# A hybrid delta-rule and attention layer on one core: three steps given more planner ticks, and a pair's triangle scaled head by head

## The chip, the cores and the metric

The kernel runs on one core of a Trainium2 chip. The metric is the device time of one execution in microseconds (us). The engines are named as in the profile: PE is TensorE, PEld its weight loads, DVE is VectorE, ACT is ScalarE, POOL is GpSimd, SP is SyncE, which issues DMAs. L311 is line 311 of the kernel before.

## What is computed

One layer of a streaming encoder: 2048 frames of width 1024, with 16 learned meta tokens ahead of them. Two token mixers run on the same input, and their outputs are gated, merged, projected and normalised. Cut to its core, the reference is:

```python
q_a,k_a,v_a,z_a,beta,dec, q_b,k_b,v_b,z_b, gate_a,gate_b = split(h @ w_in)
# A: gated delta rule, 8 heads of 128, chunks of 64
lower = strict(k_beta @ k.T * decay)                 # a triangle for each chunk and head
u, w  = solve(lower + I, [v_beta, k_beta*exp(g)])    # its unit triangular inverse
for each chunk:  v_new = u - w @ S;  o = q_dec @ S + attn @ v_new;  S = S*gl + k_dec.T @ v_new
y_a = rmsnorm(o) * silu(z_a)
# B: window attention, 16 heads of 64, 4 key/value heads, meta tokens always visible
y_b = softmax(q_b @ k_b.T - alibi, sink) @ v_b * silu(z_b)
mixed = sigmoid(gate_a) * (y_a @ w_proj_a) + sigmoid(gate_b) * (y_b @ w_proj_b)
out = layernorm(alpha * h + mixed @ w_out)
```

## The kernel before, in words

The tokens run in four blocks of 512; the first also handles the meta tokens. Products in float32 are made of three products of high and low parts, so a projection of 128 outputs for 512 tokens (`proj`, L304) is 24 matmuls of 128x512 at L311, issued in four steps of six.

The order of all engines is written by a planner. `run` (L223) walks over a list of **fill**: the projections, step by step. Each step of the fill is one **tick**: the planner first runs what is due in the background (`bg`; a generator there that says `yield 3` goes on three ticks later), then lets up to two streams take a step, each at its own rate a tick. **chain** is the delta rule's recurrence for four groups of two heads (`stage_c`), then attention. **side** prepares the groups: the products of keys and the scaled triangle `LT` (`stage_b1`), and the scores of queries with `vtok` (`stage_b2`). The triangle's inverse, the meta tokens' heads and the output transposes (`stage_y`) run in the background. Between two groups the fill begins with `until(lambda: "vtok" in gr[g])`: it yields until side has made that group's `vtok`. These ticks hold no matmul of the fill; below they are **empty ticks**, and such a place is a **boundary**.

PE takes its instructions in the order written: a matmul of the fill that stands behind a waiting transpose waits as well. What isn't fill shares four PSUM banks (`bank()`, the pool `ps`), handed out in turn; a bank that still has a reader holds back who is next.

The lines that count below: L403, L404 and L406 write the meta tokens' keys in two copies (ACT) and their low part (DVE). L492 copies the first level of the meta triangle's inverse, and L497 multiplies with it. L807 is the product of keys, L815 the scaling of the triangle, L900 the last product of a group's inverse, L920 and L933 transposes of q and v, L723 the last step of the convolved v, L935 the scaling of the transposed v by `irk`, which DVE makes by some eleven tiny steps ahead of it (L160 to L169, L926; L937 follows). L960 to L994 is the recurrence; L971 multiplies by the state, L974 subtracts, L979 multiplies by the inverse, L984 scales, L992 updates the state. L962 adds a chunk's output, L965 sums its squares, L1001 and another such tiny chain make its norm, eight L1006 apply it, L1023 transposes the result. In attention, L1126 scales the probabilities, L1140 transposes them, L1142 keeps their high part, L1147 the low part, and L1156 to L1159 multiply them with the values; L1047 makes a low part of q.

Of the kernel before, what the change touches and what calls it, by code (L numbers as in the profile page):

```python
# [15 lines left out]
AF = mybir.ActivationFunctionType  # L16
# [3 lines left out]
P = 128  # L20
# [4 lines left out]
NC4 = TB // P  # L25
NM = 16
# [49 lines left out]
def hybrid_kernel(  # L76
# [26 lines left out]
    V, A, G, T, SY = nc.vector, nc.scalar, nc.gpsimd, nc.tensor, nc.sync  # L103
# [16 lines left out]
    def nm(s):  # L120
        cnt[0] += 1
        return f"{s}_{cnt[0]}"

    def g4(shape, dt=F32):
        return gp.tile(shape, dt, tag="g", name=nm("g"))

    def y4(shape, dt=F32):
        return gp.tile(shape, dt, tag="g", name=nm("y"))

    def s2(shape, dt=F32):  # L130
        return sp.tile(shape, dt, tag="s", name=nm("s"))

    def tiny(shape, tag, bufs=None):
        if bufs is None:
            bufs = 1 if tag[0] == "m" and tag not in ("mn", "mv") or tag[:2] == "gm" and tag[-1] not in "eg" else 2
        return tp.tile(shape, F32, tag=tag, name=nm(tag), bufs=bufs)

    def bank(pool=None):
        if pool is None:
            return pp.tile([P, 512], F32, tag="ps", name=nm("ps"))  # L140
        return pool.tile([P, 512], F32, tag="acc", name=nm("acc"))

    f = lambda ap: ap.bitcast(F32)
    def split_lo(out_, src, hi, pool=False):
        eng = G if pool else V
        eng.tensor_tensor(out=out_, in0=src, in1=f(hi), op=ALU.subtract)  # L146
# [4 lines left out]
    kmt = cp.tile([P, 2, KV, NM], F32R, name="kmt")  # L151
# [47 lines left out]
    def bg(gen, after=0):  # L199

        if after:
            clock["n"] += 1
            heapq.heappush(waiting, (clock["now"] + after, clock["n"], gen))
            return
        try:
            r = next(gen)
        except StopIteration:
            return
        if callable(r):
            def poll(r=r):  # L210
                while not r():
                    yield 3
                bg(gen)
            bg(poll())
            return
        bg(gen, r)
# [6 lines left out]
    def until(cond):  # L223
        while not cond():
            yield
# [172 lines left out]
    def meta_kb(u):  # L398
        def go(pf):
            for i in range(2):  # L400
                kv = 2 * u + i
                src = pf[64 * i:64 * i + 64, :NM]
                A.activation(kmt[0:64, 0, kv, :], src, AF.Copy)  # L403
                A.activation(kmt[64:128, 0, kv, :], src, AF.Copy)  # L404
                for a in (0, 64):
                    V.tensor_tensor(out=kmt[a:a + 64, 1, kv, :], in0=src, in1=f(kmt[64 * i:64 * i + 64, 0, kv, :]), op=ALU.subtract)  # L406
        return go
# [25 lines left out]
    def meta_heads(g, mstage, ok):  # L433
# [6 lines left out]
            out=gt,  # L440
            in0=tri[:NM, :NM].unsqueeze(1).to_broadcast([NM, 2, NM]),
# [21 lines left out]
        ncj = tiny([NM, 2], "mncj")  # L463
# [3 lines left out]
        pk = bank()  # L467
# [3 lines left out]
        LT = tiny([NM, 2, NM], "mLT")  # L471
# [16 lines left out]
        for lv in (1, 2, 3):  # L488
            pz = bank()
            for hh in range(2):  # L490
                T.matmul(pz[:NM, hh * NM:hh * NM + NM], M[:, lv, hh, :], W[:, 1, hh, :], start=True, stop=True)
            A.activation(Z, pz[:NM, 0:32].rearrange("p (h i) -> p h i", h=2), AF.Copy)  # L492
            yield 2
            n = 2 if lv < 3 else 1
            pw = bank()
            for hh in range(2):
                T.matmul(pw[:NM, hh * NM:hh * NM + NM], Z[:, hh, :], W[:, 0, hh, :], start=True, stop=True)  # L497
                if n == 2:
                    T.matmul(pw[:NM, 32 + hh * NM:32 + hh * NM + NM], W[:, 0, hh, :], Z[:, hh, :], start=True, stop=True)
            V.tensor_tensor(out=W[:, 0:n], in0=W[:, 0:n], in1=pw[:NM, 0:32 * n].rearrange("p (w h i) -> p w h i", w=n, h=2), op=ALU.add)  # L500
            yield 2
# [103 lines left out]
    def block(b, nextx):  # L605
# [174 lines left out]
        def stage_b1(g):  # L780

            d, h0 = gr[g], 2 * g
            beta, eg = gates["b"], gates["eg"]
            sk = tiny([P, 2, NC4], "sk")
            ktok = g4([P, 2, NC4, P])
            for hh in range(2):
                yield from until(lambda: ("ok", "kT", hh) in d)
                kT = d["kT"]
                pk = bank()
                for c in range(NC4):  # L790
                    T.transpose(out=pk[:, c * P:(c + 1) * P], in_=kT[:, hh, c * P:(c + 1) * P], identity=ident)
                A.activation(ktok[:, hh], pk, AF.Copy)
                for c in range(NC4):
                    A.activation(junk, pk[:, c * P:(c + 1) * P], AF.Square, accum_out=sk[:, hh, c:c + 1])
                yield
            LT = g4([P, 2 * NC4, P])
            cj = tiny([P, 2, NC4], "cj", 3)
            ncj = tiny([P, 2, NC4], "ncj")
            ce = tiny([P, 2, NC4], "ce", 3)
            yield from until(lambda: "E" in d)  # L800
            E = d["E"]
            yield
            pks = [bank() for hh in range(2)]
            for hh in range(2):
                for c in range(NC4):
                    kc = kT[:, hh, c * P:(c + 1) * P]
                    T.matmul(pks[hh][:, c * P:(c + 1) * P], kc, kc, start=True, stop=True)  # L807
            V.tensor_scalar(out=sk, in0=sk, scalar1=4e-6, scalar2=None, op0=ALU.add)
            V.reciprocal(out=cj, in_=sk)
            V.tensor_tensor(out=cj, in0=cj, in1=beta[:, :, h0:h0 + 2].rearrange("p c h -> p h c"), op=ALU.mult)  # L810
            V.tensor_scalar(out=ncj, in0=cj, scalar1=-1.0, scalar2=None, op0=ALU.mult)
            V.tensor_tensor(out=ce, in0=cj, in1=eg[:, 1, :, h0:h0 + 2].rearrange("p c h -> p h c"), op=ALU.mult)
            for hh in range(2):
                for c in range(NC4):
                    V.scalar_tensor_tensor(out=LT[:, hh * NC4 + c, :], in0=pks[hh][:, c * P:(c + 1) * P], scalar=ncj[:, hh, c:c + 1],  # L815
                                           in1=E[:, hh, c * P:(c + 1) * P], op0=ALU.mult, op1=ALU.mult)
            d.update(ktok=ktok, LT=LT, sk=sk, cj=cj, ce=ce)
            bg(inverse(g))
            yield
# [193 lines left out]
        def stage_y(g):  # L1013

            d = gr[g]
            yield lambda: ("ok", "zs", 1) in d
            yield 1
            o, zs = d["o"], d["zs"]
            gr[g] = None
            for hh in range(2):  # L1020
                pt = bank()
                for c in range(NC4):
                    T.transpose(out=pt[:, c * P:(c + 1) * P], in_=o[:, hh, c, :], identity=ident)  # L1023
                V.scalar_tensor_tensor(out=zs[:, hh, :], in0=pt, scalar=gw, in1=zs[:, hh, :], op0=ALU.mult, op1=ALU.mult)
                yield 2
            yield 2
            yh = y4([P, 2, TB], F32R)
            A.activation(yh, zs, AF.Copy)
            yield 5
            yl = y4([P, 2, TB], F32R)  # L1030
            split_lo(yl, zs, yh)
            ya.append((yh, yl))
# [99 lines left out]
        def swa_turn(ch, w):  # L1132

            s = w["starts"][ch]
            Pt = w["Pt"]
            kt = (208 - s) // 2
            pT = bank()
            for j in range(2):
                for rt in range(2):
                    T.transpose(out=pT[0:kt, j * 256 + rt * P:j * 256 + rt * P + P], in_=Pt[:, ch, rt, s + j * kt:s + j * kt + kt], identity=ident)  # L1140
            ph = s2([P, 512], F32R)
            A.activation(ph[0:kt], pT[0:kt], AF.Copy)  # L1142

            def end():
                yield 1
                pl = s2([P, 512], F32R)
                V.tensor_tensor(out=pl[0:kt], in0=pT[0:kt], in1=f(ph[0:kt]), op=ALU.subtract)  # L1147
                w["p", ch] = kt, ph, pl

            bg(end())  # L1150
# [127 lines left out]
        def project(nx):  # L1278
# [125 lines left out]
            def terms(acc, c, kq, k2, wh, wl, lo):  # L1404
# [4 lines left out]
                else:  # L1409
# [6 lines left out]

        chain = series(*(stage_c(g) for g in range(4)), swa())
        side = series(decays(), stage_b0(0), *(p_ for g in range(3) for p_ in (stage_b1(g), stage_b0(g + 1), stage_b2(g))),
                      stage_b1(3), stage_b2(3), swa_first())
        both = (chain, side)  # L1420
        run([tokens(), *stage_a(0), k_b(0), k_b(1)], both, (RATES[0], SIDE[0]))
# [3 lines left out]
        u = [p_ for kv in range(1, KV) for p_ in swa_proj(kv)]  # L1425
# [102 lines left out]
```

## Time and profile before

| what | us |
|---|---|
| three runs | 2647.66, 2648.50, 2649.97 (median 2648.50) |
| the profiled execution | 2648.3 |
| its span in the trace | 2646.5 |
| PE busy in it | 2608.6 (99%) |
| DVE, ACT, POOL busy | 1533.4, 1222.9, 772.8 |

The profiled execution has 1.8 us around its span. PE is busy nearly all the time, so the table of what PE waits for is the one to read; then the timeline of PE and DVE at the places where it waits. Busy time of modelled matmuls overlaps, so starts tell more than durations.

### The profile page before, as it was taken

How to read it: one execution, taken by the hardware profiler on the slowest of the kernel's cores; microseconds unless marked ns; L12 is line 12 of the kernel's file. 1: busy time of each engine (PE TensorE's matmuls, PEld its weight loads, DVE VectorE, ACT ScalarE, POOL GpSimd, SP SyncE). 2: the span in 40 equal slices, each digit the busy share in tenths (PEclk: the TensorE clock that was granted, in tenths of full speed). 3: DMA queues.
4: the chain of work that ended last, by engine and by line, in shares of the span. 5: the costliest groups of instructions: out<-in, count | busy, mean ns of one | idle time of the engine just before them, and what ended most of it. 6: DMA issues, size and time to landing. Idle time of an engine off the chain costs nothing.

```text
span 2646.5 us, 44333 instructions
## 1 busy us (share of the span) xinstructions
PE 2608.6 (99%) x15444; PEld 2173.8 (82%) x15444; DVE 1533.4 (58%) x3863; ACT 1222.9 (46%) x3260; POOL 772.8 (29%) x1792
## 2 busy tenths in 40 slices
PE   9999999999999999999999999999999999999998
PEld 7677878888888888888888888888888888888886
DVE  6667756763565554763465554676347456476435
ACT  4565545552245544653224554565323454365422
POOL 2554333532056330111116532010102753011022
PEclk9999999999999999999999999999999999999999
DMA  7655555653675454674466545476347644557533
GB/s 257 207 198 180 186 191 159 200 167 96 205 244 169 135 167 143 201 207 132 152 225 186 170 135 164 151 212 184 120 157 243 190 142 149 164 172 210 171 98 136
DMA packets 243136, 461.61 MB, mean 174 GB/s; under 512 B 77648, under 2 KB 135760, under 8 KB 242912
## 3 DMA queue, kind: packets, MB, share of 16 engines
q1 hardware_dynamic: 242912, 458.78, 54.4%
q8 instruction: 122, 2.00, 0.3%
q14 instruction: 102, 0.84, 0.1%
HBM read 379.87 MB, written 78.81 MB: 173 GB/s over the span
## 4 chain that ended last, share of the span: by engine, by line
PE 89%; DVE 6%; ACT 3%; DMA 1%; issue 1%; SPq 0%; POOL 0%; DVEq 0%; ACTq 0%
PE acc L311 63%; PE ps L1140 2%; PE ps L1105 2%; PE ps L915 1%; PE ps L960 1%; PE ps L807 1%; PE ps L971 1%; PE ps L1158 1%; PE ps L992 1%; PE acc L1408 1%; PE acc L1411 1%; PE acc L1410 1%; PE ps L979 1%; PE ps L981 1%; PE ps L1408 1%; PE ps L1411 1%
## 5 line engine op out<-in xcount | busy, mean ns | idle before, releaser
L311 PE MATMUL acc<-xh,wh 128*128 128x512 f32 x1800 | 735.2, 408 | 0.3 <-ACT wh L275 0.3
L311 PE MATMUL acc<-xl,wh 128*128 128x512 f32 x1800 | 705.4, 392 | 0.0
L311 PE MATMUL acc<-xh,wl 128*128 128x512 f32 x1800 | 480.7, 397 | 0.0
L275 ACT ACTIVATE wh<-wr 128x1024 fp32r<-128x1024 f32 (+1 forms) x246 | 258.4, 1050 | 281.6 <-PE acc L311 151.8
L311 PEld LDWEIGHTS acc<-xh,wh 128*128 128x128 f32 x1800 | 339.1, 188 | 60.1 <-issue 1.4
L311 PEld LDWEIGHTS acc<-xl,wh 128*128 128x128 f32 x1800 | 339.7, 189 | 57.1
L311 PEld LDWEIGHTS acc<-xh,wl 128*128 128x128 f32 x1800 | 329.1, 189 | 65.6 <-issue 0.5
L718 DVE SCALAR_TENSOR_TENSOR s<-st,cw,s 128x512 f32<-128x512 f32 x288 | 229.4, 797 | 108.2 <-ACT st L713 101.2
L311 PE MATMUL acc<-y,wh 128*128 128x512 f32 x1024 | 251.5, 392 | 0.0
L146 DVE TENSOR_TENSOR wl<-wr,wh 128x1024 fp32r<-128x1024 f32 (+2 forms) x125 | 161.9, 1295 | 149.7 <-ACT wh L275 128.6
L841 POOL TENSOR_TENSOR tm<-X,g 128x60 f32<-128x60 f32 (+24 forms) x496 | 163.1, 329 | 251.8 <-DMA g<-d 216.7
L311 PEld LDWEIGHTS acc<-y,wh 128*128 128x128 f32 x1024 | 188.5, 188 | 36.7
L311 PE MATMUL acc<-xh,wr 128*128 128x512 f32 x624 | 210.7, 402 | 0.0
L1257 POOL TENSOR_TENSOR g<-g 128x512 f32<-128x512 f32 x32 | 69.7, 2177 | 395.4 <-DVE g L1250 385.5
L843 POOL TENSOR_TENSOR X<-X,tm 128x60 f32<-128x60 f32 (+24 forms) x496 | 170.8, 344 | 38.8
L1142 ACT ACTIVATE s<-ps 104x512 fp32r<-104x512 f32 (+2 forms) x128 | 76.3, 597 | 153.3 <-PE ps L1140 137.3
L1250 DVE SCALAR_TENSOR_TENSOR g<-g,acc 128x512 f32<-128x512 f32 x64 | 44.0, 687 | 154.5 <-PE acc L311 154.5
L311 PEld LDWEIGHTS acc<-xh,wr 128*128 128x128 f32 x624 | 115.6, 188 | 21.5
L311 PE MATMUL acc<-y,wl 128*128 128x512 f32 x512 | 130.7, 392 | 0.0
L146 POOL TENSOR_TENSOR wl<-wr,wh 128x256 fp32r<-128x256 f32 x120 | 87.0, 756 | 137.4 <-ACT wh L275 116.6
L760 POOL TENSOR_TENSOR g<-cm,gh 128x256 fp32r<-128x256 f32 x64 | 53.9, 872 | 249.6 <-DVE gh L672 206.9
L1241 ACT ACTIVATE g<-acc,bg__162 128x512 f32<-128x512 f32 x64 | 44.1, 689 | 177.3 <-PE acc L311 171.0
(340 smaller groups left out, 4679.6 us busy)
## 6 DMA issues: line engine op xcount, KB each, us to landing
wr<-in_wfm_dram SPq DMA_DIRECT2D x214, 512.0 KB
wl<-ws SPq DMA_DIRECT2D x165, 512.0 KB
wr<-ws SPq DMA_DIRECT2D x78, 512.0 KB
wh<-ws SPq DMA_DIRECT2D x75, 512.0 KB
ws<-wl SPq DMA_DIRECT2D x68, 512.0 KB
g<-kd SPq DMA_DIRECT2D x240, 96.0 KB
ws<-wh SPq DMA_DIRECT2D x38, 512.0 KB
wr<-in_wo_dram SPq DMA_DIRECT2D x32, 512.0 KB
```

What stands on the lines that cost most here:

```text
L146: eng.tensor_tensor(out=out_, in0=src, in1=f(hi), op=ALU.subtract)
L275: A.activation(hi[:, k], raw[:, k], AF.Copy)
L311: T.matmul(ps, w_[:, k, :], r_(k), start=(n == 0), stop=(n == 3 * NK - 1))
L718: V.scalar_tensor_tensor(out=acc, in0=st[:, 3 - d:TB + 3 - d], scalar=cw[:, s, 3 - d:4 - d], in1=acc, op0=ALU.mult, op1=ALU.add)
L760: G.tensor_tensor(out=gt[:, hh, c:c + 2], in0=tri.unsqueeze(1).to_broadcast([P, 2, P]), in1=part[:, c:c + 2, h0 + hh:h0 + hh + 1].to_broad ...
L841: G.tensor_tensor(out=tm[:, :n, :r], in0=X[:, :n, j:j + 1].to_broadcast([P, n, r]), in1=L[:, j:j + 1, j + 1:].to_broadcast([P, n, r]), op= ...
L843: G.tensor_tensor(out=X[:, :n, j + 1:], in0=X[:, :n, j + 1:], in1=tm[:, :n, :r], op=ALU.add)
L1105: T.matmul(o_, d["q", rt][:, 2 * cp2 + ch], KX[:, l, ch, s:208], start=l == 0, stop=l == 1)
L1140: T.transpose(out=pT[0:kt, j * 256 + rt * P:j * 256 + rt * P + P], in_=Pt[:, ch, rt, s + j * kt:s + j * kt + kt], identity=ident)
L1142: A.activation(ph[0:kt], pT[0:kt], AF.Copy)
L1257: G.tensor_tensor(out=m[:, u % 2, :], in0=t[:, 0, :], in1=t[:, 1, :], op=ALU.add)
L1408: T.matmul(acc, ah, wl[:, k2, :], start=False, stop=kq == 3 and k2 == 1)
```

## The change

It has five edits. (1) The meta tokens' keys: all four copies on ACT first, then the four subtractions on DVE. (2) In the first group's meta triangle, three ticks instead of two after the copy of L492. (3) In `stage_b1` the tiny steps on DVE come ahead of the products, each head takes its bank apart, and between the scalings of the first head and those of the second lies one more step of side, so that the inverse and all later steps of side come one step later for each group. (4) The output transposes come three ticks after what they wait for, instead of one. (5) The probabilities' low part is published one tick after the subtraction.

```diff
     def meta_kb(u):
         def go(pf):
             for i in range(2):
+                for a in (0, 64):
+                    A.activation(kmt[a:a + 64, 0, 2 * u + i, :], pf[64 * i:64 * i + 64, :NM], AF.Copy)
+            for i in range(2):
                 kv = 2 * u + i
                 src = pf[64 * i:64 * i + 64, :NM]
-                A.activation(kmt[0:64, 0, kv, :], src, AF.Copy)
-                A.activation(kmt[64:128, 0, kv, :], src, AF.Copy)
                 for a in (0, 64):
                     V.tensor_tensor(out=kmt[a:a + 64, 1, kv, :], in0=src, ...)
@@ meta_heads, after the copy of L492
-            yield 2
+            yield 2 + (g == 0)
@@ stage_b1
-            pks = [bank() for hh in range(2)]
-            for hh in range(2):
-                for c in range(NC4):
-                    kc = kT[:, hh, c * P:(c + 1) * P]
-                    T.matmul(pks[hh][:, c * P:(c + 1) * P], kc, kc, start=True, stop=True)
             V.tensor_scalar(out=sk, in0=sk, scalar1=4e-6, ...)
 ...
             for hh in range(2):
+                pk = bank()
                 for c in range(NC4):
+                    kc = kT[:, hh, c * P:(c + 1) * P]
+                    T.matmul(pk[:, c * P:(c + 1) * P], kc, kc, start=True, stop=True)
+                if hh:
+                    yield
+                for c in range(NC4):
-                    V.scalar_tensor_tensor(out=LT[:, hh * NC4 + c, :], in0=pks[hh][:, c * P:(c + 1) * P], ...)
+                    V.scalar_tensor_tensor(out=LT[:, hh * NC4 + c, :], in0=pk[:, c * P:(c + 1) * P], ...)
             d.update(ktok=ktok, LT=LT, sk=sk, cj=cj, ce=ce)
             bg(inverse(g))
@@ stage_y, ahead of the output transposes
-            yield 1
+            yield 3
@@ swa_turn, end
                 V.tensor_tensor(out=pl[0:kt], in0=pT[0:kt], in1=f(ph[0:kt]), op=ALU.subtract)
+                yield 1
                 w["p", ch] = kt, ph, pl
```

Since the order is planned, the edits move more than the lines they touch. Lines of the changed kernel stand one to three further down (L971 is L973 there, L1023 is L1025). Its planner runs 1511 ticks instead of 1487, six more in each block, of which 36 instead of 12 are empty: four instead of two at each boundary of block 0, and four, two and two instead of two, none and none in each later block.

On PE at the third boundary of block 0, the kernel before ends the inverse, transposes v twice and goes on with the fill (`acc`; `cm` with a `g` is a transpose):

```order
L900 MATMUL ps_2935<-g_1520,s_2868 64x64 x8
L933 MATMUL ps_2967<-cm,g_2779 128x128 x4
L933 MATMUL ps_3012<-cm,g_2779 128x128 x4
L311 MATMUL acc_3028<-xh_101,wh_2849 128x512
L311 MATMUL acc_3028<-xl_102,wh_2849 128x512
```

On PE, four fill matmuls, the state's product L971 and four more of the fill later, it comes to the first output transposes:

```order
L311 MATMUL acc_3028<-xh_126,wh_2849 128x512
L311 MATMUL acc_3028<-xl_127,wh_2849 128x512
L317 MATMUL acc_3054<-wr_2692,xm 32x128 x8
L1023 MATMUL ps_3066<-cm,g_1140 128x128 x4
L311 MATMUL acc_3028<-xh_132,wh_2849 128x512
```

On PE at the same place, the changed kernel (L902 is before's L900, L922 its L920, L935 its L933; `S` is the state):

```order
L311 MATMUL acc_2831<-xh_132,wl_2708 128x512 x2
L902 MATMUL ps_2911<-g_1518,s_2847 64x64 x8
L922 MATMUL ps_2957<-cm,g_2518 128x128 x4
L935 MATMUL ps_2994<-cm,g_2769 128x128 x4
L973 MATMUL ps_3009<-S_86,g_1393 128x128 x2
L1025 MATMUL ps_3016<-cm,g_1157 128x128 x4
L935 MATMUL ps_3028<-cm,g_2769 128x128 x4
L311 MATMUL acc_3044<-xh_101,wh_2828 128x512
```

The output transposes now stand in the empty ticks, right behind the state's product, with no fill between them and the inverse's last product; the second half of v's transposes stands behind them.

On DVE in the fourth group of block 0, the kernel before ends the chain for `irk`, then v's last step (L723), then begins the norm of the outputs (L1001):

```order
L169 SCALAR_TENSOR_TENSOR irk_3881<-rst_3885,irk_3881 128x8
L926 TENSOR_TENSOR irk_3881<-irk_3881,sk_3076 128x8
L937 TENSOR_SCALAR sq_3661<-sq_3661 128x8
L723 SCALAR_TENSOR_TENSOR g_3797<-s_3875,s_3793 128x512
L1001 SCALAR_TENSOR_TENSOR so_3041<-so_3041,sq_1737 128x8
L160 TENSOR_SCALAR rsi_3928<-so_3041 128x8
```

On DVE at the same place, the changed kernel from the end of the norm's chain (`ro`) on:

```order
L169 SCALAR_TENSOR_TENSOR ro_3870<-rst_3874,ro_3870 128x8
L1008 TENSOR_SCALAR g_2000<-g_2000,ro_3870 128x128 x8
L160 TENSOR_SCALAR rsi_3899<-sk_3101 128x8
L161 TENSOR_SCALAR irk_3898<-rsi_3899 128x8
L167 SCALAR_TENSOR_TENSOR rst_3902<-sk_3101,irk_3898 128x8
```

On DVE, after six more rows of that chain:

```order
L169 SCALAR_TENSOR_TENSOR irk_3898<-rst_3902,irk_3898 128x8
L928 TENSOR_TENSOR irk_3898<-irk_3898,sk_3101 128x8
L939 TENSOR_SCALAR sq_3675<-sq_3675 128x8
L724 SCALAR_TENSOR_TENSOR g_3795<-s_3896,s_3789 128x512
L146 TENSOR_TENSOR wl_3850<-wr_3733,wh_3848 128x1024
```

The norm and its eight scalings (L1008) now stand ahead of the chain for `irk`, and v's last step (L724) stands last of all three.

On DVE at the start of attention in block 0, the kernel before (`ls` are the sums of the first and the second set of probabilities):

```order
L1121 TENSOR_TENSOR ls_5132<-ls_5132,m_949_5131 128x4
L1122 RECIPROCAL ls_5132<-ls_5132 128x4
L1126 TENSOR_SCALAR g_5129<-g_5129,ls_5132 128x80 x2
L1126 TENSOR_SCALAR g_5129<-g_5129,ls_5132 128x144 x2
L1047 SCALAR_TENSOR_TENSOR g_5238<-acc_5159,g_5238 64x8x64 x2
L1121 TENSOR_TENSOR ls_5193<-ls_5193,m_964_5192 128x4
L1122 RECIPROCAL ls_5193<-ls_5193 128x4
L1126 TENSOR_SCALAR g_5190<-g_5190,ls_5193 128x208 x4
L1147 TENSOR_TENSOR s_5289<-ps_5270,s_5275 40x512
```

On DVE at the same place, the changed kernel:

```order
L1049 SCALAR_TENSOR_TENSOR g_5232<-acc_5137,g_5232 64x8x64 x2
L1123 TENSOR_TENSOR ls_5150<-ls_5150,m_954_5149 128x4
L1124 RECIPROCAL ls_5150<-ls_5150 128x4
L1128 TENSOR_SCALAR g_5147<-g_5147,ls_5150 128x80 x2
L1128 TENSOR_SCALAR g_5147<-g_5147,ls_5150 128x144 x2
L1123 TENSOR_TENSOR ls_5199<-ls_5199,m_964_5198 128x4
L1124 RECIPROCAL ls_5199<-ls_5199 128x4
L1128 TENSOR_SCALAR g_5196<-g_5196,ls_5199 128x208 x4
L1149 TENSOR_TENSOR s_5295<-ps_5276,s_5281 40x512
```

The two steps for the low part of q (L1047, L1049 there) moved from between the two sets to ahead of both.

## Rows read from the trace of the kernel before

**Rows 1.** The page: its head, and part 1, busy time by engine.

```profile
span 2646.5 us, 44333 instructions
PE 2608.6 (99%) x15444; PEld 2173.8 (82%) x15444; DVE 1533.4 (58%) x3863; ACT 1222.9 (46%) x3260; POOL 772.8 (29%) x1792
```

**Rows 2.** PE's waits: its line, whom it waited for; total us, times, longest.

```profile
PE acc L629 <- ACT wh L275: 4.6, 1, 4.6
PE ps L992 <- DVE s L984: 3.1, 3, 1.0
PE ps L1158 <- DVE s L1147: 2.6, 5, 1.6
PE ps L915 <- ACT g L889: 1.8, 3, 0.6
...
PE ps L1023 <- DVE g L1006: 1.2, 1, 1.2
PE ps L1023 <- DVE s L1147: 1.1, 3, 0.4
...
PE ps L497 <- ACT g L492: 1.0, 1, 1.0
...
PE ps L979 <- ACT g L430: 0.8, 1, 0.8
...
PE acc L311 <- ACT wh L275: 0.3, 1, 0.3
```

**Rows 3.** Timeline, start of attention in block 0: start, us, engine, line, operation, tiles [idle before].

```profile
428.42 1.39 DVE L1047 SCALAR_TENSOR_TENSOR g<-acc,g 64x512 fp32r<-64x512 f32 x2
...
433.70 0.59 PE L1158 MATMUL ps<-s,s 40*64 40x256 f32 x2 [1.62 <-DVE s L1147]
...
434.43 2.93 PE L311 MATMUL acc<-xh,wl 128*128 128x512 f32 x6
```

**Rows 4.** Windows there: stretch, length, busy us by engine, PEclk, DMA share, GB/s.

```profile
433.80:437.30 3.50, 3.50 (x10) 2.69 (x11) 3.12 (x18) 0.00 (x0) 0.40 (x3) 0.51 0.85 283
```

**Rows 5.** Timeline, third boundary of block 1.

```profile
907.53 2.32 DVE L718 SCALAR_TENSOR_TENSOR s<-st,cw,s 128x512 f32<-128x512 f32 x3
...
910.25 0.68 PE L992 MATMUL ps<-s,g 128*128 128x128 f32 x4 [1.04 <-DVE s L984]
...
910.69 1.63 PE L311 MATMUL acc<-xh,wl 128*128 128x512 f32 x6
```

**Rows 6.** Timeline, third boundary of block 0.

```profile
229.09 0.29 DVE L416 TENSOR_TENSOR macc<-mstage,cw 128x32 f32<-128x32 f32 x1
...
230.71 1.34 DVE L146 TENSOR_TENSOR wl<-wr,wh 128x1024 fp32r<-128x1024 f32 x1
...
231.37 1.14 PE L900 MATMUL ps<-g,s 64*64 64x64 f32 x16
...
232.44 1.09 PE L933 MATMUL ps<-cm,g 128*128 128x128 f32 x8
...
232.91 0.17 DVE L160 TENSOR_SCALAR rsi<-sk 128x8 int32<-128x8 int32 x1
...
235.44 0.15 DVE L1001 SCALAR_TENSOR_TENSOR so<-so,sq 128x8 f32<-128x8 f32 x1
...
238.00 1.93 DVE L1006 TENSOR_SCALAR g<-g,ro 128x128 f32<-128x128 f32 x8
...
238.54 0.88 PE L1023 MATMUL ps<-cm,g 128*128 128x128 f32 x4 [1.21 <-DVE g L1006]
```

**Rows 7.** Timeline, fourth group of block 0.

```profile
300.40 0.30 DVE L424 SCALAR_TENSOR_TENSOR mkm<-mth,macc 128x32 f32<-128x32 f32 x1
...
303.94 0.70 DVE L723 SCALAR_TENSOR_TENSOR g<-s,s 128x512 f32<-128x512 f32 x1 [0.40 <-ACT s L721]
...
305.87 0.60 PE L933 MATMUL ps<-cm,g 128*128 128x128 f32 x4
```

**Rows 8.** All 128 of L815: ns min/median/max, first and last start, tiles.

```profile
L815 DVE SCALAR_TENSOR_TENSOR g<-ps,ncj,g x128: 335/342/353, 65.6 to 2209.9; 128x128 f32<-128x128 f32 x128
```

More of the change, by code (lines that the diff above doesn't have):

```diff
@@ L813, in stage_b1 @@
             for hh in range(2):
+                pk = bank()
                 for c in range(NC4):
-                    V.scalar_tensor_tensor(out=LT[:, hh * NC4 + c, :], in0=pks[hh][:, c * P:(c + 1) * P], scalar=ncj[:, hh, c:c + 1],
+                    kc = kT[:, hh, c * P:(c + 1) * P]
[3 more added lines that the diff above has]
+                for c in range(NC4):
+                    V.scalar_tensor_tensor(out=LT[:, hh * NC4 + c, :], in0=pk[:, c * P:(c + 1) * P], scalar=ncj[:, hh, c:c + 1],
                                            in1=E[:, hh, c * P:(c + 1) * P], op0=ALU.mult, op1=ALU.mult)
```

## Prediction

> **What bounds the kernel now.** I read the page first: PE is busy 2608.6 of 2646.5 us, and DVE, ACT and POOL are busy for less than 60% [rows 1]. So a change that adds no matmul can give back only what PE waits, and can cost only new waits. Then I read the table of PE's waits: of its nineteen rows, from 4.6 to 0.3 us and 25.2 us in all, the largest is the first weight at the program's start, which no edit reaches [rows 2]. Last I read the timeline where PE waits. Two things are to be seen there. Most waits last 1.2 us or less, and they are places where a chain of tiny steps on DVE or a copy on ACT is a little longer than the work that PE has ahead of it. One is longer: in block 0 the low part of the probabilities holds PE for 1.62 us, and right behind it six matmuls of the fill take 2.93 us [rows 3]. In that stretch the granted clock is 0.51, half of the full 2.4 GHz [rows 4]. Behind a wait of 1.04 us six such matmuls took 1.63 [rows 5], so that one brought no slow stretch. So this wait cost 1.62 us, and the slow clock some 1.3 to 1.7 more (2.93 less 1.63, or half of 3.50).
>
> **The change part by part.** Its 24 more ticks cost nothing by themselves: an empty tick holds no matmul, PE takes the next thing in its row. What counts is that each empty tick takes away six matmuls, 1.63 us of cover [rows 5], from whatever PE waits for next. I worked each place from the new order and the durations of the trace.
>
> Block 0, first boundary. The third tick after L492 and the copies in a new order put other work between the copy and L497. Its wait of 1.0 [rows 2] goes: **-1.0** (0 to -1.5; the other waits of that inverse may grow or go).
>
> Block 0, second boundary. L979 now follows closer on L974, which DVE reaches behind a chain of tiny steps. The nearest row is the wait at L979 for ACT, 0.8 [rows 2]: **+0.8** (0 to 1.5).
>
> Block 0, third boundary. In the new order DVE runs, from where the seven tiny steps of the meta convolution began (229.09), first L146 (1.34 [rows 6]), a 128x512 step (0.7, as L723 [rows 7]), then these seven (229.09 to 230.71, 1.62), then the norm's chain (235.44 to 238.00, 2.56) and eight L1006 (1.93) [rows 6]. So the first L1006 is done at about 235.5, the fourth at 236.3, the eighth at 237.2. PE comes to the output transposes after L900 (231.37, 1.07 to the next start) and twelve short matmuls or transposes (some 1.3; eight L933 took 1.09 [rows 6]), at 233.7. Instead of running until 234.1 they end at 236.4: 2.3 lost. Behind the norm DVE then makes `irk` (232.91 to 235.44, 2.53 [rows 6]) and L974 (two of some 0.34 as L815 [rows 8]), until 240.4. PE has four transposes and six matmuls for that time (0.5 and 1.63 [rows 5, 6]) and stands at L979 from 238.5 to 240.4: 1.9 lost. Edit (4) means to clear this, but its three ticks are empty ones here. Less the 1.21 of L1023 in the kernel before [rows 6]: **+3.0** (+1 to +6: the one end if DVE comes to the chain 2 us sooner, the other if the copies of L935, which free the bank that L979 takes, end later).
>
> Block 0, fourth group. The second half of v's transposes (L933 at 305.87, no wait) needs L723, done at 304.6 [rows 7]. In the new order DVE has the norm's chain, eight L1006 and the chain for `irk` first: from the end of L424 (300.7 [rows 7]) 2.56 + 1.93 + 2.53 [rows 6] + 0.7 [rows 7] = 7.7, so 308.4. PE has the same work ahead: **+2.6** (+1 to +5, since the squares that the norm needs may come later).
>
> Block 0, the clock. The last three of these waits are 2.3, 1.9 and 2.6 us long, and the only row for a wait of such a length had the half clock behind it [rows 3, 4]. One such stretch at 1.5 is in the sum (0 to 4.8, none or all three): **+1.5**. The Trainium skill, page "TensorE: Matmul & The Clock Gate", section "HAM oscillation — how this bites in real kernels", says that an engine that idles long enough between pieces of work falls to the low clock and works slowly again after each such gap, so that the price of a gap is more than the gap; that speaks against this change, which makes one gap into three. By that rule all three would pay, 3 us on top of my sum; the trace agrees with it at 433.70 [rows 3, 4], and shows no gap of this length without it.
>
> Block 0, attention. Here the reason that the 1.62 us go is not the tick of edit (5) but the shift of the whole plan: L1047 (1.39 [rows 3]) moved from between the two sets of probabilities to ahead of both, so L1147 stands 1.39 sooner behind its set. The wait falls to some 0.2, and with it the slow stretch: -1.4 - 1.6 = **-3.0** (-3.5 to 0: if other work on DVE moved into the gap, nothing is gained). The other four waits of L1158 (1.0 in all [rows 2]) and edit (5)'s tick give **-0.5** more. In the steady state a set passes every five ticks and the order of PE and DVE is the same as before, so this tick costs nothing: the transposes, scores and values of the sets around lie between as they did.
>
> Blocks 1 to 3, each. L992's wait of 1.0 goes, since the empty ticks shift the recurrence past the three L718 (2.32 us) that held L984 [rows 5], but one of about the same size comes at the same boundary, where L979 has two ticks less ahead of it and DVE still has a norm to make: 0. L915's wait of 0.6 goes [rows 2], and 0.3 of L1023's behind L1147 [rows 2]: edit (4) moves these transposes two ticks on. In the last group the split triangle has a cost: the bank for L979 is freed by L962, which DVE now reaches behind L146 (1.34 [rows 6]), L723 (0.7), five tiny steps (0.2 each, as the seven above) and the four scalings of the first head (4 x 0.342 = 1.37 [rows 8]), 4.4 us; PE has some 3.2 of fill and the eight products (1.1 if they take what eight L933 do [rows 6]) in that time, and DVE starts only when L971 has landed: +0.4 (0 to 1.2). The scalings of the second head, the inverse and the recurrence one step later cost nothing as long as the recurrence doesn't wait for its inverse; the fill covers that, but at a boundary nothing does (this is in the +0 to +1.2). Sum for a block **-0.5** (-1.5 to +2), for three **-1.5**.
>
> The sum: -1.0 + 0.8 + 3.0 + 2.6 + 1.5 - 3.0 - 0.5 - 1.5 = **+1.9**. The profiled execution took 2648.3 (2646.5 in the span [rows 1] and 1.8 around it), 0.2 under the median of 2648.5. So 2650.2.
>
> **The rivals.** *Slower, by the clock.* Each of the three new gaps of block 0 is followed by half clock as the one of 1.62 us was, and two of them stand at their upper ends: 3 x 1.6 instead of 1.5 (+3.3), +4.5 instead of +3.0, +4.5 instead of +2.6: 2650.2 + 6.7 = 2656.9. For it speak the rows at 433.70 [rows 3, 4]; against it that DVE may come to its chains earlier than I put it, since it is busy for 58% only. It decides from 3.6 us above my sum, which is two stretches of half clock and a little of the gaps.
>
> *Faster.* The orders at the boundaries are not as tight as I read them, no new wait forms, and the old ones go: 1.62 and 1.6 for the clock, 1.0 for L1158's others, 1.1 and 1.2 for L1023, 1.0 for L497, 1.8 for L915, part of L992's 3.1 (say 1) [rows 2]: -10.3, so 2638. For it speaks that each edit stands at a wait of the table; against it that the new ticks are empty ones just where the norm is late, and that nearly all of the list has to go to get 5.3.
>
> *The change doesn't do what it says.* The output transposes' ticks are empty, edit (5)'s leaves the order as it is, and the step of `stage_b1` is made up by side's rate; only small waits move about: 2648 to 2649.
>
> **How the numbers follow.** A measurement of this kernel can tell about 0.2% from no change, 5.3 us: under 2643.2 is faster, over 2653.8 slower. My forecast, new gaps in block 0 that just outweigh what goes, has 0.42; the rival without effect 0.20; slower by the clock 0.25; faster 0.13. The forecast's own bounds (2645 to 2654) lie within 0.2% but for a little, so: faster 0.13, same 0.61, slower 0.26. The range leaves out the far half of each of the two outer rivals: 2643.5 to 2657.
>
> **What would show it.** In the profile after: at the third boundary of block 0, waits of L1025 for L1008 and of L981 for L976 or L937 of about 2 us each; in the fourth group, one of L935 for L724 of 2 to 3 us; half clock behind at least one of them. The wait of L1161 for the low part at 433 gone, and PEclk 1.00 there. In blocks 1 to 3, L915's and L992's waits gone, new ones at L981. If PE's waits in block 0 sum to less than before, the order of DVE didn't bind where I said; if the sum of PE's waits fell but the time didn't, the clock took it.

## The result, and the profile after

The changed kernel is **slower by 1.3%**: 2682.9 us median (2679.5 to 2685.0) against 2648.1, a ratio of 1.013 with a 95% interval of 1.0115 to 1.0145. The forecast was 2650.2, with a range up to 2657.0, so the time lies 26 us outside of it. The profiled execution has a span of 2679.8, 33.3 more than before [rows 1].

The page of the changed kernel, its head and part 1:

```profile
span 2679.8 us, 44360 instructions
## 1 busy us (share of the span) xinstructions
PE 2620.7 (98%) x15444; PEld 2188.3 (82%) x15444; DVE 1544.1 (58%) x3863; ACT 1223.0 (46%) x3260; POOL 777.1 (29%) x1792
```

PE runs the same 15444 instructions, yet is busy for 12.1 us longer than before [rows 1]. This goes with the slow clock: the mean granted clock is 0.990 instead of 0.998, and ahead of the program's end the trace has half clock in eight stretches of 41 us in all, where the kernel before has one of 3.4. The rest of the 33 us is waiting. PE's waits in the changed kernel (its line, whom it waited for; total us, times, longest):

```profile
PE acc L311 <- DMA wh<-ws: 9.1, 2, 4.7
PE ps L792 <- DVE g L724: 5.4, 7, 1.3
PE acc L311 <- ACT carry L716: 5.2, 1, 5.2
...
PE ps L935 <- DVE g L724: 3.1, 1, 3.1
PE ps L1025 <- DVE g L1008: 2.5, 1, 2.5
PE ps L981 <- DVE s L976: 2.1, 3, 0.7
PE ps L1142 <- DVE s L1149: 2.1, 1, 2.1
PE ps L513 <- DVE s L509: 1.7, 1, 1.7
PE ps L451 <- POOL mgt L440: 1.5, 1, 1.5
...
PE ps L981 <- ACT g L937: 1.1, 1, 1.1
```

The whole table adds up to 46.1 us, 20.9 more than before; with the 12.1 of PE's busy time this is the 33 us. L1158, L992, L915 and L497 of [rows 2] are gone, smaller or moved, as forecast (the lines are one to three higher here; L792 is before's L791, the transposes of k). The waits of L935, L1025 and L981 are those that the prediction worked out. L792's, 3.9 us more than before's L791, aren't in it. Nor are the largest, the first and the third row: the **fill itself** waits for 4.4, 5.2 and 4.7 us, once in each of blocks 1 to 3. (The third row names an ACT copy that ended last. But the load of the same weights is complete at 1475.51 there, 0.14 us ahead of PE's start, just as in the two others.)

Comparing the starts of the same L311 in both traces tells where the time went: block 0 is 16.6 us longer, block 1 by 4.2, block 2 by 7.1, block 3 by 4.9.

How a weight comes late shows in the timeline of SP's queue and POOL. The changed kernel, first group of block 1 (L831 stores the triangle's diagonal blocks, L835 loads them in another layout, POOL solves them in L843 and L845, L851 stores the result X, L856 loads it back, L256 loads weights):

```profile
779.60 1.81 SPq L831 DMA_DIRECT2D d<-g  x4
781.51 0.40 SPq L256 DMA_DIRECT2D wh<-ws  x1
782.00 0.38 SPq L256 DMA_DIRECT2D wl<-ws  x1
782.72 1.72 SPq L835 DMA_DIRECT2D g<-d  x4
...
790.16 0.24 POOL L843 TENSOR_TENSOR tm<-X,g 128x31 f32<-128x31 f32 x1 [12.97 <-DMA g<-d]
...
819.30 2.78 SPq L851 DMA_DIRECT2D d<-X  x4
...
823.57 1.81 SPq L856 DMA_DIRECT2D XT<-d  x4
825.43 0.45 SPq L256 DMA_DIRECT2D wh<-ws  x1
...
829.22 0.47 PE L311 MATMUL acc<-xh,wh 128*128 128x512 f32 x1 [4.43 <-DMA wh<-ws]
```

The same place in the kernel before, whose lines there are L829, L833, L841, L849 and L854:

```profile
760.23 1.82 SPq L829 DMA_DIRECT2D d<-g  x4
763.35 1.71 SPq L833 DMA_DIRECT2D g<-d  x4
765.10 0.42 SPq L256 DMA_DIRECT2D wh<-ws  x1
765.57 0.43 SPq L256 DMA_DIRECT2D wl<-ws  x1
...
767.57 0.53 POOL L841 TENSOR_TENSOR tm<-X,g 128x31 f32<-128x31 f32 x1 [7.61 <-DMA g<-d]
...
795.81 2.54 SPq L849 DMA_DIRECT2D d<-X  x4
...
799.84 1.82 SPq L854 DMA_DIRECT2D XT<-d  x4
801.70 1.90 SPq L256 DMA_DIRECT2D wh<-ws  x1
```

At the block's start the changed kernel is 16.8 us late. Less that, the store of the blocks is 2.6 us later (779.60 to 760.23): the step of side that edit (3) adds ahead of the inverse. But POOL begins 5.8 later (790.16 to 767.57), because the plan now puts a pair of weight loads between the store and the load of the blocks, and the blocks' transfer stands behind 1 MB of weights. X is stored 6.7 later. The store waits **in SP's queue** until POOL is done, and behind it stand the weights of a fill that is not late. So they are issued 6.9 us later than in the kernel before. PE stands for 4.4 of these, so the kernel before had some 2.5 us to spare here (6.9 less 4.4).

SP's own waits for the two stores, changed kernel first:

```profile
SPq L851 <- POOL X L845: 85.0, 11, 15.0
SPq L831 <- DVE g L817: 61.9, 10, 7.6
```

The kernel before:

```profile
SPq L829 <- DVE g L815: 47.3, 8, 8.7
SPq L849 <- POOL X L843: 41.0, 7, 8.5
...
SPq L829 <- DVE XN L860: 18.1, 4, 4.7
```

In the kernel before this queue was already held for 41 us by the store of X, with no row among PE's waits that told of it. The store of X is the one that grew, to 85 us. The store of the blocks did not in all: before it had two rows, 65.4 us together, against 61.9.

### The profile page after: what moved, and what is told of

Same layout as the page of the kernel before. It is cut to its first block, busy times and chain, and to the rows that moved or that the text cites. A ratio compares the mean times of both kernels' runs of the same rounds, so it can differ in the third digit from the quotient of the medians.

```text
span 2679.8 us, 44360 instructions
## 1 busy us (share of the span) xinstructions
PE 2620.7 (98%) x15444; PEld 2188.3 (82%) x15444; DVE 1544.1 (58%) x3863; ACT 1223.0 (46%) x3260; POOL 777.1 (29%) x1792
## 4 chain that ended last, share of the span: by engine, by line
PE 81%; DVE 6%; POOL 4%; DMA 3%; ACT 2%; issue 2%; SPq 1%; DVEq 0%; POOLq 0%; ACTq 0%
PE acc L311 57%; PE ps L1142 2%; PE ps L1107 2%; POOL tm L843 2%; POOL X L845 2%; DVE s L719 2%; PE ps L962 1%; PE ps L1161 1%; PE ps L981 1%; PE ps L994 1%; PE ps L973 1%; PE ps L983 1%; PE acc L1414 1%; PE acc L1411 1%; PE acc L1413 1%
## 5 line engine op out<-in xcount | busy, mean ns | idle before, releaser
L311 PE MATMUL acc<-xh,wh 128*128 128x512 f32 x1800 | 742.5, 412 | 15.7 <-DMA wh<-ws 9.1
L311 PE MATMUL acc<-xl,wh 128*128 128x512 f32 x1800 | 712.9, 396 | 0.0
L311 PE MATMUL acc<-xh,wl 128*128 128x512 f32 x1800 | 482.6, 398 | 0.0
L311 PEld LDWEIGHTS acc<-xh,wh 128*128 128x128 f32 x1800 | 343.3, 191 | 78.7 <-issue 10.9
L311 PEld LDWEIGHTS acc<-xl,wh 128*128 128x128 f32 x1800 | 344.2, 191 | 58.2
L311 PEld LDWEIGHTS acc<-xh,wl 128*128 128x128 f32 x1800 | 331.3, 190 | 66.0 <-issue 0.5
L843 POOL TENSOR_TENSOR tm<-X,g 128x60 f32<-128x60 f32 (+24 forms) x496 | 169.2, 341 | 291.3 <-DMA g<-d 256.0
L311 PE MATMUL acc<-y,wh 128*128 128x512 f32 x1024 | 253.1, 393 | 0.0
L311 PEld LDWEIGHTS acc<-y,wh 128*128 128x128 f32 x1024 | 188.2, 188 | 36.3
L311 PE MATMUL acc<-xh,wr 128*128 128x512 f32 x624 | 210.4, 403 | 0.0
L845 POOL TENSOR_TENSOR X<-X,tm 128x60 f32<-128x60 f32 (+24 forms) x496 | 169.9, 343 | 38.9
L311 PEld LDWEIGHTS acc<-xh,wr 128*128 128x128 f32 x624 | 115.9, 188 | 21.6
L311 PE MATMUL acc<-y,wl 128*128 128x512 f32 x512 | 130.6, 392 | 0.0
L1080 POOL CAST g<-kmt 128x32 fp32r<-128x32 f32 x128 | 26.2, 236 | 347.5 <-PE ps L973 179.3
```

The source lines that it names most:

```text
L311: T.matmul(ps, w_[:, k, :], r_(k), start=(n == 0), stop=(n == 3 * NK - 1))
L843: G.tensor_tensor(out=tm[:, :n, :r], in0=X[:, :n, j:j + 1].to_broadcast([P, n, r]), in1=L[:, j:j + 1, j + 1:].to_broadcast([P, n, r]), op= ...
L845: G.tensor_tensor(out=X[:, :n, j + 1:], in0=X[:, :n, j + 1:], in1=tm[:, :n, :r], op=ALU.add)
```

## The experiments

All ratios are to the kernel before, with a 95% interval. Lines are those of each kernel.

**Edit (3) alone, and all but edit (3).** The first kernel has the part `@@ stage_b1` of the diff shown above, the second has all other parts.

> The kernel before with edit (3) alone: the split triangle with its extra step of side. Theory A (the extra step moves the inverse's DMAs and POOL's loop later, and SP's queue then holds weight loads back): nearly the whole loss is here, 2672 to 2688 us, with three waits of L311 for its weights of 4 to 5.5 us, one in each of blocks 1 to 3, and block 0 some 10 to 18 us longer. Rival B (the loss is shared out over the five edits, since each adds ticks): 2655 to 2668, and waits of L311 below 2 us.

Measured: 2684.2 us (1.0133, 1.0118 to 1.0148). L311 waited 5.3, 7.3 and 9.1 us, two of them longer than theory A allowed, and block 0 was 14 us longer.

> All edits but (3). Theory A: 2638 to 2650 us, no wait of L311 for weights in blocks 1 to 3, no wait of L935 for L724 in the fourth group. Rival B: 2655 to 2668 us, with waits of L1025 and L513 in block 0 that stay.

Measured: 2653.5 us (1.0022, 1.0012 to 1.0031). No wait of L311 over 0.7 in blocks 1 to 3, none of L935 for L724. So the split alone makes the whole loss, with longer waits for weights than beside the other edits. The other four cost 5 us together, 3.5 above the top of what theory A allowed; see the runs of single edits.

**The split without its step.**

```
-                if hh:
-                    yield
```

> The changed kernel without the extra step between the first and the second head's scalings; the tiny steps stay ahead of the products and each head takes its bank apart. Theory A: the step is what costs, the order on DVE and the banks are worth under 2 us: 2638 to 2650 us. Rival C (the order on DVE, with the tiny steps and the scalings behind L719 and L724, makes the scaled triangle late and with it the inverse): more than half of the loss stays, 2664 us or more.

Measured: 2653.9 us (1.0019, 1.0009 to 1.0029), as without the split, and 3.9 above theory A's top like that one. The step alone makes the loss; the banks and the order of the tiny steps cost nothing that can be measured beside the other edits. Rival C falls.

**The store of X behind one more pair of weights.** `DMA` holds the ticks between the inverse's steps; the fourth lies ahead of the store.

```
-DMA = (1, 3, 4, 1, 2, 7)
+DMA = (1, 3, 4, 5, 2, 3)
```

> The changed kernel with one set of waits of the inverse moved: the store of X is issued four ticks later and the copy after its return four ticks sooner, so that one more pair of weight loads stands ahead of the store in SP's queue; nothing else is moved. Theory A: the three waits of L311 (4.4, 5.2 and 4.7 us) shrink below 1.5 us each and the slow clock behind them goes: 2658 to 2670 us. Rival D (the weights come late because the transfers are slow or because their buffers are free too late, not because of the queue): the waits stay, 2678 us or more.

Measured: 2661.1 us (1.0045, 1.0030 to 1.0060), 21.8 us less than the changed kernel. Its waits of PE, the first rows:

```profile
PE ps L792 <- DVE g L724: 5.1, 7, 1.2
PE acc L630 <- ACT wh L275: 4.5, 1, 4.5
PE ps L917 <- ACT junk L924: 3.1, 5, 2.2
PE ps L935 <- DVE g L724: 3.0, 1, 3.0
PE ps L1025 <- DVE g L1008: 2.5, 1, 2.5
```

No row of L311 for weights is left, and nothing was changed but the places of X's store and load back among the weights in SP's queue. The transfers were not slow and the buffers not late: rival D falls. Block 0 stays 13.8 us longer, so its loss is another one. Blocks 1 and 3 are now 0.9 and 2.0 us shorter than before. Block 2 is still 4.7 longer: L917 waits there for 2.2 us, with 6 us at half clock behind it.

**The load of the blocks ahead of a pair of weights, and the norm behind L724.** Two kernels, each from the changed one:

```
-DMA = (1, 3, 4, 1, 2, 7)
+DMA = (1, 1, 6, 1, 2, 7)
```

```
-            bg(end(), 1)
+            bg(end(), 1 + 5 * (first and g == 1))
```

> The changed kernel with one wait of the inverse two ticks shorter and the next two ticks longer: the load of the triangle's blocks (L835) is again issued ahead of a pair of weight loads in SP's queue, as in the kernel before; POOL's loop keeps its place in the plan. Theory A: in blocks 1 to 3 POOL's loop begins some 3 us sooner and the three waits of L311 (4.4, 5.2, 4.7) shrink to 0 to 2.5 each: 2664 to 2675 us. Rival E (the extra step of side alone makes the loop late, and the pair ahead of the load costs nothing): the waits stay above 4, 2678 us or more.

Measured: 2672.5 us (1.0090, 1.0075 to 1.0106), 10.4 less than the changed kernel. The waits shrink to 3.6, 2.6 and 3.4, more than theory A allowed for. The place of the load among the weights is thus about a third of these waits; the rest went only without the extra step, or with the store of X further back.

> The changed kernel with the norm of the second group's outputs in block 0 four ticks later, so that on DVE L724 stands ahead of it again; on PE only that group's two output transposes move. Theory F (a gap of 3 us brings the slow clock, so it costs more than itself): the wait of 3.1 us of L935 for L724 goes and with it the slow stretch of 9 us behind it: 5.5 to 8 us less than the changed kernel, 2675 to 2677.5. Rival G (the slow clock there has another cause, or the gap only moves to the next reader): 0 to 3.5 us less, with PEclk about 0.5 still after 318.

Measured: 2677.0 us (1.0106, 1.0091 to 1.0121), 5.9 less. The wait of L935 is gone. Between the fill's matmuls on both sides of the place the saving is 7.1 us, for a wait of 3.1. The changed kernel there, timeline and then a window with its clock (stretch, length, busy us by engine, PEclk, DMA share, GB/s):

```profile
313.31 1.99 DVE L1008 TENSOR_SCALAR g<-g,ro 128x128 f32<-128x128 f32 x8
...
317.70 0.68 DVE L724 SCALAR_TENSOR_TENSOR g<-s,s 128x512 f32<-128x512 f32 x1
...
318.44 1.11 PE L935 MATMUL ps<-cm,g 128*128 128x128 f32 x4 [3.13 <-DVE g L724]
...
319.21 2.91 PE L311 MATMUL acc<-xh,wl 128*128 128x512 f32 x6
```

```profile
318.40:327.90 9.50, 9.46 (x38) 7.23 (x39) 2.24 (x5) 4.05 (x11) 7.93 (x26) 0.50 0.58 188
```

The kernel with the norm behind L724, a window at the same place:

```profile
318.00:330.00 12.00, 12.00 (x68) 8.85 (x67) 8.69 (x30) 3.96 (x10) 10.37 (x30) 1.00 0.43 141
```

The slow clock went with the gap: theory F holds, and this gap of 3.1 us cost 7. Over all of block 0 the two profiled executions differ by 2.9 us only: up to this place PE, DVE, ACT and POOL have the same order in both kernels, and yet the second one was 4 us behind by then. Single executions can differ by that much in block 0, so a difference of a few us in its length says little.

**Edits alone.** Edit (5), edit (4), and edits (1) with (2), each in the kernel before, as their parts of the diff stand above.

> The kernel before with edit (5) alone. Theory H (the tick moves the values behind the transposes of the next set, so the 1.62 us of L1158 go and a wait of about 2 us of the probabilities' transposes for L1147 takes their place): 2647 to 2651 us. Rival I (edit (5) carries the 5 us that the edits without the split cost): 2652 to 2655 us.

Measured: 2649.0 us (1.0003, 0.9993 to 1.0012). Neither theory: the wait at 433 stays at 1.63 us as it was. The edit leaves that order as it is, as one of the prediction's rivals said. And the same gap has full clock behind it here, where the kernel before had half [rows 3, 4]:

```profile
433.23 0.45 PE L1159 MATMUL ps<-s,s 40*64 40x256 f32 x2 [1.63 <-DVE s L1147]
```

```profile
433.30:436.80 3.50, 3.50 (x21) 2.99 (x22) 3.09 (x18) 1.38 (x3) 0.43 (x3) 1.00 0.86 286
```

> The kernel before with edit (4) alone. Theory J (the output transposes only move by two ticks): the wait of 1.2 us at the third boundary shrinks, the bank waits move, 2645 to 2649 us. Rival K (the transposes later hold L429, L993 and L311 in block 0, as seen without the split): 2650 to 2654 us, with waits of L311 for ACT of 1 to 2 us near 335.

Measured: 2653.7 us (1.0020, 1.0011 to 1.0029). Rival K's time, but not its place: no wait of L311 near 335. In each later block L992 waits 1.41 instead of the 1.04 of [rows 5] and L791 some 0.45, and in block 0 a wait of 1.28 at L428 takes the place of L1023's 1.21 [rows 6]. These rows give some 2 of the 5 us; where the others are stays open.

> The kernel before with edits (1) and (2) alone. Theory: the wait of 1.0 us of L497 goes and little else moves, 2646 to 2649 us. Rival: the meta heads later by a tick hold the recurrence of block 0 and a wait of 2 us or more of L429 or L513 shows: 2650 to 2653 us.

Measured: 2650.4 us (1.0012, 1.0002 to 1.0022), the rival's time, but not its place. L497's wait is gone, that of L492 (before's L491) grows to 1.4, and a wait of 2.7 for POOL at L451 is new; L429 and L513 wait for less than 1 us. (This profiled execution took 4.9 us more than the median, so not all of its rows are typical.)

**The inverse late alone, and side late alone.** The first is the changed kernel without the last step of `stage_b1`; the second is the kernel before with one step more there.

```
             bg(inverse(g))
-            yield
```

```
             bg(inverse(g))
             yield
+            yield
```

> The changed kernel without the last step of side in the split, so that only the second head's scalings and the inverse come a step later, and vtok and the later steps of side at their old places. Theory M (block 0's loss of 15 us comes from side's later steps and the empty ticks at the boundaries, the waits for weights from the late inverse): block 0 is some 8 to 13 us shorter, the waits of L311 remain at 1 to 4 us, since one pair now stands ahead of the copy back: 2656 to 2670 us. Rival N (the late inverse makes both): block 0 stays 12 us or more longer than before, 2672 us or more.

Measured: 2658.4 us (1.0041, 1.0026 to 1.0056). Block 0 is as long as before (0.4 us more), and L311 waits 1.5, 4.1 and 2.4. Theory M as to block 0; rival N falls.

> The kernel before with one more step of side behind the inverse's start, and nothing else: products, scalings and inverse at their old places, vtok and the later steps of side one step later. Theory M: block 0 is 6 to 13 us longer, with waits at the third boundary and at L934 for L723, and waits of L311 for weights stay below 1.5 us: 2655 to 2665 us. Rival N: within 0.2% of the kernel before.

Measured: **2698.2 us** (1.0195, 1.0179 to 1.0210), far above both. Block 0 is 23.8 us longer, as M says though twice its size, with waits of 3.7 (L791), 3.6 (L450) and 3.1 (L934). But blocks 1 to 3 are some 8.4 longer each, and there M was wrong: in each, L311 waits 3.0 to 3.3 us for weights and L972 some 2.2, with half clock behind both. SP's queue and PE in that kernel:

```profile
822.33 2.56 SPq L850 DMA_DIRECT2D d<-X  x4
824.98 1.02 SPq L256 DMA_DIRECT2D wr<-ws  x2
```

```profile
829.31 0.47 PE L311 MATMUL acc<-xh,wr 128*128 128x512 f32 x1 [3.04 <-DMA wr<-ws]
```

Here the inverse is at its old place. But the store of X, planned a fixed number of ticks ahead, comes one pair of weights **sooner** in SP's queue, since more of these ticks are empty and the weights go by the fill; and that pair (`wr`) is the one that waits. So the same queue loses time in two ways: POOL later at the same place in the queue, or the same POOL with the store further up.

The gap at L934 in block 0 of this kernel is as long as the one that cost 7 us above, and stands ahead of the same transposes of v. Yet the clock behind it is full:

```profile
326.17 0.66 PE L934 MATMUL ps<-cm,g 128*128 128x128 f32 x4 [3.07 <-DVE g L723]
```

```profile
326.20:330.00 3.80, 3.80 (x19) 2.95 (x20) 2.73 (x4) 2.98 (x7) 3.50 (x12) 1.00 0.55 166
```

**All repairs together, and what beats both.**

> The changed kernel with the three repairs of the former runs together: the load of the triangle's blocks ahead of a pair of weight loads, the store of X behind one, and the norm of the second group's outputs in block 0 behind L724. If theory A and F hold and their savings don't overlap elsewhere: 17 to 20 us less by the queue, 6 by the norm, so 2656 to 2661 us, with no wait of L311 over 0.5 us in blocks 1 to 3. Rival: the savings overlap or other waits open, 2664 us or more.

The changed kernel with `DMA = (1, 1, 6, 5, 2, 3)` and the norm behind L724. Measured: 2651.7 us (1.0013, 1.0004 to 1.0022), 31 us less than the changed kernel and 4 below the expected bounds. Block 0 is 5.8 us longer than before, but each later block 2 us **shorter**.

> Edits (3), (4) and (5) with the two repairs of SP's queue in blocks 1 to 3 alone; in block 0 only the order of the tiny steps, the banks and the meta copies are changed. If the loss of block 0 comes from its boundaries alone, and the edits gain some 2 us in each later block once no weight waits behind the store: 2640 to 2645 us, with PE's waits in blocks 1 to 3 that sum to 1 us less each than in the kernel before. Rival (the gain of the later blocks in the former run was the repairs of the queue alone, or the noise of one execution): 2646 to 2650 us.

Edits (3) to (5) only where `first` is false (in block 0 no step in the split and the old ticks), edit (2) left out, and the repaired `DMA` in blocks 1 to 3. Measured: **2642.2 us** (0.9976, 0.9966 to 0.9985), 6.5 us below the kernel before. The page's busy times:

```profile
PE 2603.5 (99%) x15444; PEld 2174.6 (82%) x15444; DVE 1537.0 (58%) x3863; ACT 1222.9 (46%) x3260; POOL 778.8 (30%) x1792
```

Block 1 as a window, in the kernel before and then in this one:

```profile
724.81:1365.13 640.32, 637.49 (x3689) 536.56 (x3688) 356.23 (x893) 291.56 (x777) 161.76 (x412) 1.00 0.55 172
```

```profile
723.59:1361.87 638.28, 635.85 (x3689) 537.02 (x3688) 357.64 (x893) 291.50 (x777) 164.78 (x412) 1.00 0.55 173
```

> The kernel before with the two repairs of SP's queue in blocks 1 to 3 and nothing else. If the kernel before has slack at that store (it shows no wait of L311 for weights in blocks 1 to 3): within 2 us of the kernel before, 2646 to 2650 us. Rival (the earlier load of the triangle's blocks makes the recurrence of the later blocks sooner and so saves its waits): 2640 to 2645 us.

The kernel before with the same `DMA` in blocks 1 to 3. Measured: 2648.8 us (1.0000, 0.9991 to 1.0009). So the gain belongs to the edits, once no weight waits behind the store. In the kernel with the edits each later block is 2.0 to 2.3 us shorter. Only 0.4 to 0.8 of this are PE's waits, less than the 1 us that was expected. The other 1.6 are PE's busy time, at full clock in both windows. In the whole kernel the busy time falls by 5.1 us (2608.6 [rows 1] to 2603.5), at the same mean clock of 0.998. So most of the gain isn't in the waits that the edits were aimed at. Which detail of the order makes PE's busy time shorter wasn't tried.

## Why the prediction was wrong, point by point

**The step that failed** is the last one on blocks 1 to 3: "The scalings of the second head, the inverse and the recurrence one step later cost nothing as long as the recurrence doesn't wait for its inverse; the fill covers that". It followed the inverse to PE and stopped there. The inverse also goes through SP's queue four times, which is shared with all weights. The term was 0 to +1.2 a block; the runs showed 4.4 to 5.2 us of waiting and a slow stretch behind it, at a place where PE had not waited before. Moving the store of X and its load back behind one more pair of weights, and nothing else, gave back 21.8 us.

**The other term that was far off** is block 0, +3.4 in the sum (-1.0 + 0.8 + 3.0 + 2.6 + 1.5 - 3.0 - 0.5), 16.6 measured. By the starts of the same L311, the changed kernel is some 5.5 us late before the third boundary, 10 after it and 15 after the fourth group, where the terms of the sum give -0.2, 2.8 and 5.4 without the clock. The mechanism was right, chains of tiny steps on DVE that lose their cover in empty ticks, and two of its sizes were good: the fourth group's wait was put at 2.6 and was 3.1, and the third boundary's first one at 2.3 and was 2.5. Its second one, put at 1.9, was 1.1. The rest was mis-sized:

- The clock had 1.5 us for all of block 0. PE's busy time says 12.1 for the whole kernel; the stretch behind the 3.1 us gap alone lasted 9.5 us at half clock and cost some 4, not 1.5. Block 0 has four more stretches with a granted clock of 0.50 to 0.51, of 3.4 us each, from 88.9 (L492's gap), 136.7 (L513), 242.5 (L1025) and 457.5 (L1142). The one stretch of [rows 4] was taken for the size of all, and one such stretch for their number.
- The first and second boundary were put at -1.0 and +0.8. The wait of L497 went as forecast, and that of L981 at the second boundary didn't come. But L492 ahead of L497 waits 1.5 (before's L491 0.9), and behind it come waits of 1.1 (L311), 1.7 (L513) and 1.5 (L451) that weren't foreseen: they are places of the meta heads too.
- Attention was put at -3.5, with 1.6 of it for the slow stretch of [rows 4]. Of the 1.62 us 0.3 are left (put at 0.2), by the order shown ahead of the prediction, but 6 us behind that place L1142 waits 2.1 for L1149, whose bank it takes. Half clock follows this gap as it did the old one. Between the fill's matmuls on both sides, that part is 2.2 us longer, not shorter. That the slow stretch goes with the 1.62 us was not certain either: with edit (5) alone the gap stayed and the half clock didn't come.

**The rivals.** Slower by the clock had the right sign and one of the right reasons, at 2656.9. (It spoke of two gaps at their upper ends but priced both at 4.5, where their ranges end at 6 and 5.) The queue wasn't in it either. The rule of the Trainium skill that was weighed there (page "TensorE: Matmul & The Clock Gate", section "HAM oscillation — how this bites in real kernels") was the better guide for the changed kernel: the gaps of 3.1, 4.4, 5.2 and 4.7 us each have half clock behind them in the trace, which the sum had for only one gap. The gap of 2.5 us at the third boundary has it too, 0.50 from 242.5 to 245.9. But a gap doesn't always bring it: the 1.5 us at L451 in the changed kernel, the 1.63 with edit (5) alone and the 3.07 with side late alone have full clock behind them. What decides stays open here, so a price for the clock is one that may or may not be paid. "The change doesn't do what it says" holds for edit (5) alone, within 0.2%.

Blocks 1 to 3 without the queue were right in sign: -0.5 each forecast, some -2 measured once the queue was repaired. L915's waits went, and L992's went for L981 (0.7 a block), much as the prediction had it, and for L792 (some 1.1), which it didn't have. But most of the -2 is PE's shorter busy time, for which the prediction had no term: to that extent the right sign was luck.

## What to carry to other kernels

Where one queue issues both the transfers of a side computation and the operands of the main stream, a step that moves the side computation has to be followed into that queue: ask what the queue waits for at each of its transfers, who stands behind it, and how much slack those have. A delay that is counted in ticks holds nothing back where the ticks are empty: it covers nothing there, and a transfer that is planned by it moves up in the queue, while the work that it waits for takes as long as ever. Look at SP's waits even where PE's table shows no row for them: 41 us in the kernel before were a few us away from the critical path.

## What the runs showed of the hardware

In the changed kernel a gap of 3.1 us on PE was followed by 9.5 us at half the clock, although PE was busy in 9.46 of them, and cost 7.1 us in all; a gap of 1.62 us had 3.5 us at half clock behind it [rows 3, 4]. The length of the gap alone didn't tell: 1.63 us at the same matmuls, with edit (5) alone, and 3.07 us, with side late alone, were followed by a granted clock of 1.00. The load of the triangle's blocks, issued behind two weight loads of 512 KB each, let POOL start 7.4 us after its issue (782.72 to 790.16), and 4.2 us where it was issued ahead of them (763.35 to 767.57). The changed kernel with nothing but the load moved ahead has 4.1 there (780.89 to 784.95).
